# A fixed TensorE order in the recurrence groups of a bidirectional RWKV-7 layer: value products ahead of the lora-ups, bonus sums one key product later

## The chip, the cores and the metric

One core of a Trainium2 chip runs the whole kernel. The metric is the device time of one execution in microseconds. Five engines matter here: TensorE (PE, with its weight loads shown as PEld), VectorE (DVE), ScalarE (ACT), GpSimd (POOL), and SyncE (SP), whose queue issues most DMA transfers. Each engine works through its own list of instructions in order; semaphores tie the lists together.

## The reference

One layer over 2176 tokens (128 context tokens, 2048 latent ones) of 1024 channels. All tokens go through one input projection to eight groups of 512 channels. Four of them (r, k, v and a gate) feed an RWKV-7 recurrence, the other four a short convolution. For the recurrence the reference computes, cut to what matters here:

```python
proj = h @ lp['w_in']
r, k, v, g_a, b_gate, c_gate, u_conv, g_b = jnp.split(proj, IN_SPLITS, axis=-1)
rkv = _token_shift(jnp.concatenate([r, k, v], axis=-1), mu, is_latent)   # mixes each token with its two neighbours
lw = jnp.tanh(h @ decay_down);  w = decay_w0 + lw @ decay_up             # per direction
decay = jnp.exp(-jnp.exp(-softplus(-w) - 0.5))
a = sigmoid(iclr_bias + (h @ iclr_down) @ iclr_up)                       # per direction
kk = heads(k * kk_scale);  kk = kk * rsqrt(max(sum(kk * kk, -1), 1e-24))
kd = k * (1 + (a - 1) * ka_scale)                                        # per direction
# ... the recurrence itself, over r, decay, kd, v, kk, a ...
bonus = sum(r * kd * bonus_rk, axis=(direction, head channel))
y = y + bonus * v
```

## The kernel before

The kernel has a first phase, which makes the recurrence's operands and the convolution half and spills them to DRAM, and later phases, which run the recurrence and the output projection. Only the first phase is touched.

**Blocks, thirds, groups.** The tokens are cut into six blocks j of 384 tokens (the last has 256), and the blocks into three thirds of two (`THIRD`). For each third the loop goes over four groups g of 128 channels, and inside over the third's two blocks: `groupA(g, j, ...)` makes the recurrence operands of one group and block. There are 24 such calls. After the four groups of a third come its four convolution groups (`groupB`).

**A product** (`dense`) is a 128-channel slice of the projection for one block: eight slices of the 1024 input channels, three matmuls each (high and low parts of an fp32 split), so 24 matmuls into one PSUM tile. The tiles are named mmk, mmr, mmv and mmg for key, receptance, value and gate. The PSUM pool `pmm` has five buffers in turn, shared by these four and by the four lora-ups of a group (`up`, two matmuls each), eight tiles a group.

**A token shift** (`shifted`) evacuates a product: ScalarE copies it into a padded tile (rawl; for the context, which is in block 0, rawc too) and scales it (q1k, q1r, q1v), GpSimd adds the two neighbours (shk, shr, shv), and VectorE joins both (ok, or, ov, the shifted key, receptance and value).

**A part sum** (`part_sum`) adds the channels of each head with a matrix of ones: ScalarE copies the input to a high part (hsh), GpSimd subtracts it from the input (hsl, the low part), and TensorE does two matmuls. A group has two: the *key sum* pss of the squared key (sq, parts hshs and hsls), whose maximum and reciprocal VectorE takes for the normalised key; and the *bonus sum* psb of bs, a product of both directions' kd and the shifted receptance (parts hshb and hslb). bs is written into the first kd tile, so it shows as `kd<-kd,dv,or`.

**The rest of a group.** Per direction: tanh of the two lora-ups, a scan over 64 tokens (t), two exponentials (pp and t), and four operand tiles al, rh, ka and be, all with the tag "sp" and four buffers in turn, each spilled by a DMA from SP's queue; a ninth "sp" tile q takes bonus times value. Three transposes (psv) turn the value, VectorE subtracts its mean (vmean, vt) and vt is spilled. The low part of a part sum and vt share one buffer (tag "vt").

**Order.** A scheduler with a cost model of its own puts each engine's instructions in order from the program's order and its estimates, so that an engine's list need not follow the text. In the first third the weights are split into their parts when first loaded (`load_w`: a cast on ScalarE, a subtraction on VectorE) and written back; the later thirds read the parts.

Of the kernel before, what the change touches and what calls it, by code (L numbers as in the profile page):

```python
# [49 lines left out]
def phase1(K):  # L50
# [50 lines left out]
    def dcol(i):  # L101
        return dv[:, i:i + 1]
# [84 lines left out]
            q = 32 * (k % 4)  # L187
            T.matmul(ps[q:q + 32, :], scp[:, k, :], wt[:, i, :], start=k < 4, stop=k >= 4)

    def parts_of(t_, n, nm, eng):  # L190

        hi = ta_.tile([128, 384], F32R, tag="hsh", name=f"hsh{nm}", bufs=1)
        lo = ta_.tile([128, 384], F32R, tag="vt", name=f"hsl{nm}", bufs=1)
        P.copy(hi[:, :n], t_[:, :n])
        eng.tensor_tensor(lo[:, :n], t_[:, :n], hi[:, :n].bitcast(F32), ALU.subtract)  # L195
        return hi, lo

    def part_sum(o, t_, n, nm, eng=G):

        hi, lo = parts_of(t_, n, nm, eng)  # L200
        ps = pax.tile([128, 384], F32, tag="ax", name=f"ps{nm}")
        T.matmul(ps[:, :n], o[:], hi[:, :n], start=True, stop=False)
        T.matmul(ps[:, :n], o[:], lo[:, :n], start=False, stop=True)
        return ps
# [123 lines left out]
    def groupA(g, j, ws, hh, lw, pre):  # L328
# [8 lines left out]
        P.activation(sq[:, :n], kS[:, :n], AF.Square, scale=vcol(V_KK + g))  # L337
        pss = part_sum(onr, sq, n, f"s{g}_{j}")
# [4 lines left out]
        P.activation(kk[:, :n], kS[:, :n], AF.Identity, scale=vcol(V_KK + g))  # L343
        kkn = n2
        V.tensor_tensor(kkn[:, :n], kk[:, :n], n2[:, :n], ALU.mult)
        rS = shifted(psr or dense(wr_, hh, n, "r"), j, 0, g, "r", 1)
        kds = []
        for d in range(2):
            cs = slice(g * 128, g * 128 + 128)
# [23 lines left out]
            ta = tl("ta", 2)  # L373
            P.activation(ta[:, :n], psa[:, :n], AF.Tanh, bias=dcol(D_IBH + d * 4 + g), scale=0.5)  # L374
            v3 = lambda x_: x_[:, :n].rearrange("p (a b) -> p a b", b=64)
            al = tl("sp", 4)
            V.tensor_tensor(v3(al), v3(kk), pt[:, :nch, d:64 + d], ALU.mult)
            spill(f"al{d}", g, j, al, "al")
            rh = tl("sp", 4)
# [4 lines left out]
            kd = tl("kd", 2)  # L384
            P.activation(kd[:, :n], ta[:, :n], AF.Identity, bias=dcol(D_KA2 + g), scale=vcol(V_KA + g))
            V.tensor_tensor(kd[:, :n], kd[:, :n], kS[:, :n], ALU.mult)
            kap = tl("sp", 4)
            V.tensor_tensor(kap[:, :n], kd[:, :n], c[:, :n], ALU.mult)
            spill(f"ka{d}", g, j, kap, "kap")
            be = tl("sp", 4)  # L390
            V.scalar_tensor_tensor(be[:, :n], ta[:, :n], 1.0, kkn[:, :n], ALU.add, ALU.mult)
            V.tensor_tensor(be[:, :n], be[:, :n], c[:, :n], ALU.mult)
            spill(f"be{d}", g, j, be, "be")
# [1 line left out]
        bs = kds[0]  # L395
        V.tensor_tensor(bs[:, :n], kds[0][:, :n], kds[1][:, :n], ALU.add)
        V.scalar_tensor_tensor(bs[:, :n], bs[:, :n], dcol(D_RKQ + g), rS[:, :n], ALU.mult, ALU.mult)
# [18 lines left out]
        psg = dense(wg, hh, n, "g")  # L416
        tg = tl("sg", 2)
        P.activation(tg[:, :n], psg[:, :n], AF.Tanh, scale=0.5)
        sg = tg
        V.scalar_tensor_tensor(sg[:, :n], tg[:, :n], 1.0, psg[:, :n], ALU.add, ALU.mult)  # L420
        spill("sg", g, j, sg, "sg")
        q = tl("sp", 4)
        V.tensor_tensor(q[:, :n], psb[:, :n], vS[:, :n], ALU.mult)
        V.scalar_tensor_tensor(q[:, :n], q[:, :n], dcol(D_GBH + g), sg[:, :n], ALU.add, ALU.mult)
        spill("q", g, j, q, "q")

    def groupB(g, j, ws, hh):
        t0, n = BLK[j]
# [102 lines left out]
            yield  # L531

    up = {}

    def run(gen):
        for _ in gen:
# [990 lines left out]
```

## Time and profile before

| | |
|---|---|
| three timed runs | 1683.29 us median (1681.29 to 1694.95) |
| the profiled execution | 1692.05 us, span 1690.3 us |
| recurrence groups of the first, second, last third | 69 to 237, 405 to 590, 744 to 886 us |
| share of the span: PE, DVE, ACT, POOL | 91%, 68%, 47%, 31% |
| granted TensorE clock, mean | 0.964 |
| HBM traffic | 184 GB/s over the span |

The profile is of one execution. In its rows a group of instructions is named by line, engine, operation and tiles (out<-in); a wait is put down to what ended it. Matmuls overlap, so a matmul's duration is longer than the step from one to the next. A tile's name without numbers stands for all its buffers.

### The profile page before, as it was taken

To read this page: it belongs to the slowest core of one execution; us is meant where nothing else is said; L and a number is where in the kernel's file an instruction comes from. 1 tells how busy PE (TensorE), PEld (TensorE's weight loads), DVE (VectorE), ACT (ScalarE), POOL (GpSimd) and SP (SyncE) were. 2 spreads that over 40 slices of the span, in tenths; PEclk is the share of its full clock that TensorE was granted. 3 is DMA by queue.
4 is the path that set the end of the run, shared out by engine and by line. 5 is a ranking of instruction groups with operands and counts; after the bars stand their busy time and mean duration, and the time that the engine had idled before them with its cause. 6 is when DMAs were issued, how large, how long until landed. Compare 5 with 4: busy or idle time off the path is not lost.

```text
span 1690.3 us, 42026 instructions
## 1 busy us (share of the span) xinstructions
PE 1538.1 (91%) x17364; PEld 1416.5 (84%) x17364; DVE 1147.6 (68%) x2112; ACT 792.4 (47%) x1590; POOL 531.6 (31%) x952
## 2 busy tenths in 40 slices
PE   5898899999999899999999998998989897699998
PEld 2898899898888899999998997888888786577786
DVE  5988897644678744547876426798898887446433
ACT  4565554322355512225552106877867767422222
POOL 0032220000122200002321714788777775212221
PEclk9999999999999999999999998999999999899999
DMA  9688886664878763448877636566565754455442
GB/s 373 225 241 241 236 253 229 225 213 161 176 172 193 198 177 114 141 153 200 214 233 265 208 113 154 153 179 166 177 175 163 184 142 144 113 156 180 145 149 93
DMA packets 204591, 313.95 MB, mean 186 GB/s; under 512 B 58088, under 2 KB 147560, under 8 KB 190320
## 3 DMA queue, kind: packets, MB, share of 16 engines
q1 hardware_dynamic: 168816, 311.13, 61.1%
q10 hardware_dynamic: 35584, 0.14, 1.5%
q8 instruction: 136, 2.23, 0.6%
q14 instruction: 55, 0.45, 0.1%
HBM read 208.05 MB, written 103.17 MB: 184 GB/s over the span
## 4 chain that ended last, share of the span: by engine, by line
PE 46%; DVE 8%; DMA 7%; issue 3%; ACT 2%; POOL 0%; SPq 0%; DVEq 0%; ACTq 0%; POOLq 0%
PE psE L1066 6%; PE psS L1097 4%; PE psu L1381 3%; DMA scr_ops<-sp 3%; PE psu L1382 3%; PE psu L1383 3%; PE psFm L899 2%; PE psX L1048 2%; PE psGm L899 2%; PE mmb L160 1%; PE mmb L158 1%; PE mmb L159 1%; PE mmgb L159 1%; PE mmgb L160 1%; PE mmgb L158 1%
## 5 line engine op out<-in xcount | busy, mean ns | idle before, releaser
L971 POOL TENSOR_TENSOR zt<-zt,ztmp 128x30 f32<-128x30 f32 (+7 forms) x510 | 206.2, 404 | 39.7
L968 POOL TENSOR_TENSOR ztmp<-ab,zt 128x60 f32<-128x60 f32 (+7 forms) x255 | 137.2, 538 | 105.2 <-DVE ab L959 86.3
L1097 PE MATMUL psS<-sv,E 128*64 128x64 f32 x2176 | 103.1, 231 | 26.5 <-DVE so L1123 12.4
L1097 PEld LDWEIGHTS psS<-sv,E 128*64 128x64 f32 x2176 | 85.3, 141 | 46.1 <-issue 18.3
L314 POOL TENSOR_TENSOR shk<-rawl 128x384 f32<-128x384 f32 (+1 forms) x24 | 20.3, 845 | 274.8 <-ACT rawl L310 176.6
L1071 DVE TENSOR_TENSOR E<-psE,msk 128x512 f32<-128x512 f32 x136 | 91.0, 684 | 19.1 <-PE psE L1066 18.2
L1123 DVE TENSOR_TENSOR sv<-psS,pc 64x128 f32<-64x128 f32 x254 | 64.1, 275 | 42.4 <-PE psS L1097 40.8
L1446 POOL TENSOR_TENSOR z<-z,x 128x512 f32<-128x512 f32 x32 | 42.8, 1338 | 150.8 <-DVE z L1440 86.5
L158 PE MATMUL mmv<-h,w 128*128 128x384 f32 (+1 forms) x192 | 70.5, 367 | 19.6 <-ACT q1r L312 10.1
L1052 ACT ACTIVATE stf<-psX 64x512 f32<-64x512 f32 x136 | 80.5, 592 | 13.3 <-PE psX L1048 10.9
L159 PE MATMUL mmv<-h,w 128*128 128x384 f32 (+1 forms) x192 | 68.7, 358 | 0.0
L160 PE MATMUL mmv<-h,w 128*128 128x384 f32 (+1 forms) x192 | 68.5, 357 | 0.1
L195 POOL TENSOR_TENSOR hsls<-sq,hshs 128x384 fp32r<-128x384 f32 (+1 forms) x24 | 33.0, 1373 | 112.1 <-DMA scr_vt<-vt 39.5
L158 PE MATMUL mmg<-h,w 128*128 128x384 f32 (+1 forms) x192 | 63.2, 329 | 4.6 <-ACT ta L374 2.6
L158 PE MATMUL mmc<-h,w 128*128 128x384 f32 (+1 forms) x192 | 64.1, 334 | 0.5 <-DMA w<-scr_wsp 0.5
L159 PE MATMUL mmgb<-h,w 128*128 128x384 f32 (+1 forms) x192 | 63.5, 331 | 0.0
L158 PE MATMUL mmgb<-h,w 128*128 128x384 f32 (+1 forms) x192 | 63.5, 331 | 0.0
L160 PE MATMUL mmgb<-h,w 128*128 128x384 f32 (+1 forms) x192 | 63.2, 329 | 0.0
L159 PE MATMUL mmc<-h,w 128*128 128x384 f32 (+1 forms) x192 | 63.0, 328 | 0.0
L160 PE MATMUL mmb<-h,w 128*128 128x384 f32 (+1 forms) x192 | 62.8, 327 | 0.0
L160 PE MATMUL mmc<-h,w 128*128 128x384 f32 (+1 forms) x192 | 62.8, 327 | 0.0
L158 PE MATMUL mmu<-h,w 128*128 128x384 f32 (+1 forms) x192 | 62.7, 327 | 0.0
(311 smaller groups left out, 5114.4 us busy)
## 6 DMA issues: line engine op xcount, KB each, us to landing
w<-scr_wsp SPq DMA_DIRECT2D x68, 1024.0 KB, 6.8
scr_wsp<-w SPq DMA_DIRECT2D x34, 1024.0 KB, 6.1
rr<-scr_ops SPq DMA_DIRECT2D x32, 1024.0 KB, 5.6
scr_ops<-sp SPq DMA_DIRECT2D x160, 192.0 KB, 5.3
wr<-in_win SPq DMA_DIRECT2D x34, 512.0 KB, 7.0
x<-in_x SPq DMA_DIRECT2D x17, 512.0 KB, 3.6
wadas<-in_wada SPq DMA_DIRECT2D x8, 1024.0 KB, 14.8
sv<-scr_vt SPq DMA_DIRECT2D x32, 256.0 KB, 4.3
```

What stands on the lines that cost most here:

```text
L158: T.matmul(ps[:, :n], w[:, 0, k], hh[:, 0, k, :n], start=k == 0, stop=False)
L159: T.matmul(ps[:, :n], w[:, 0, k], hh[:, 1, k, :n], start=False, stop=False)
L160: T.matmul(ps[:, :n], w[:, 1, k], hh[:, 0, k, :n], start=False, stop=k == 7)
L899: T.matmul(dst(h, a, er), w[hr_, u, :], x(hr_, u), start=True, stop=True)
L968: G.tensor_tensor(tv, ab[:, j:j + 2, j + 2:32].unsqueeze(1).broadcast_to((128, kn, 2, n)), zt[:, :kn, j:j + 2].unsqueeze(3).broadcast_to(( ...
L971: G.tensor_tensor(zt[:, :kn, j + 2:32], zt[:, :kn, j + 2:32], tv[:, :, r], ALU.subtract)
L1052: P.activation(g.fs[64:128, :, hd, e::2], g.ps["X"][e][hr_].rearrange("p a (b t) -> p b a t", b=2), AF.Copy, scale=-1.0)
L1066: T.matmul(pe[r, i, hd, :].rearrange("p (b t) -> p b t", b=2), lt[:, b, hd, us.start + k + i], rt[:, :, hd, us.start + k + i], start=True, ...
L1071: V.tensor_tensor(g.E[n][:, k:k + 2].rearrange("p a b c -> p (a b) c"), pe[:].rearrange("p a b c -> p (a b) c"), B.msk[:, ME[g.d]].unsquee ...
L1097: T.matmul(g.sp[i // 4][r, q, hd, :], g.E[n][:, k, hd, r], g.sv[:, u, hd, :], start=True, stop=True)
L1123: V.tensor_tensor(dst, g.sp[i // 4][0:64, q], B.pc[0:64, d, 2 * p:2 * p + 2, c:c + 1].broadcast_to((64, 2, 64)), ALU.mult)
L1381: T.matmul(ps[:], mh[:, n], hi[:, cs], start=start and n == 0, stop=False)
```

## The change

Five edits, all in the first phase's recurrence groups:

1. Around each group's two blocks the scheduler is switched off for TensorE (`manual_schedule`), which then takes its instructions in program order.
2. In the program, receptance and value (product and shift) move up to right behind the key, ahead of the key sum and the lora-ups; the gate product moves up ahead of the value's transposes.
3. The bonus sum's two copies stay with the group, but its matmuls and q are put into `later` and come after the next group's key product (after the last group of a third, at its end).
4. The parts get homes of their own: the key sum's low part the tag "hsl", the bonus sum's two parts the tags "ob" and "bsv" of another pool, vt the tag "pv".
5. The "sp" tiles have five buffers instead of four.

```diff
-    def parts_of(t_, n, nm, eng):
-        hi = ta_.tile([128, 384], F32R, tag="hsh", name=f"hsh{nm}", bufs=1)
-        lo = ta_.tile([128, 384], F32R, tag="vt", name=f"hsl{nm}", bufs=1)
+    def parts_of(t_, n, nm, eng, home=None):
+        pool, th_, tl_ = home or (ta_, "hsh", "hsl")
+        hi = pool.tile([128, 384], F32R, tag=th_, name=f"hsh{nm}", bufs=1)
+        lo = pool.tile([128, 384], F32R, tag=tl_, name=f"hsl{nm}", bufs=1)
...
-        kS = shifted(psk or dense(wk, hh, n, "k"), j, 1, g, "k", 1)
+        psk = psk or dense(wk, hh, n, "k")
+        for f in later:
+            f()
+        later.clear()
+        kS = shifted(psk, j, 1, g, "k", 1)
+        psr = psr or dense(wr_, hh, n, "r")
+        rS = shifted(psr, j, 0, g, "r", 1)
+        psv_ = dense(wv, hh, n, "v")
+        vS = shifted(psv_, j, 2, g, "v", 1)
...
-        rS = shifted(psr or dense(wr_, hh, n, "r"), j, 0, g, "r", 1)
...
-            al = tl("sp", 4)
+            al = tl("sp", 5)
...
-        psb = part_sum(onr, bs, n, f"b{g}_{j}")
-        vS = shifted(dense(wv, hh, n, "v"), j, 2, g, "v", 1)
+        bp = parts_of(bs, n, f"b{g}_{j}", G, (tp, "ob", "bsv"))
+        psg = dense(wg, hh, n, "g")
...
-        vt = ta_.tile([128, 3, 128], F32, tag="vt", name=f"vt{g}_{j}", bufs=1)
+        vt = tp.tile([128, 3, 128], F32, tag="pv", name=f"vt{g}_{j}", bufs=1)
...
+        def bonus():
+            psb = sum_of(onr, bp, n, f"b{g}_{j}")
+            q = tl("sp", 5)
...
+        later.append(bonus)
...
+            order = tc.manual_schedule(engines={mybir.EngineType.PE})
+            order.__enter__()
             for j in js:
                 groupA(g, j, ws, hs[j], lws[j], pre.pop(j, None))
+            if g == 3:
+                for f in later:
+                    f()
+                later.clear()
+            order.__exit__(None, None, None)
```

`sum_of` is the second half of `part_sum`: the PSUM tile and the two matmuls.

How the lists of three engines change is shown at one place, the pass from block 2 to block 3 in the second group of the second third (`_2_` and `_3_` are the blocks). TensorE before, from the bonus sum of block 2 (psb) inside the key product of block 3:

```order
L202 MATMUL psb_2_4415<-hshb_2_4411,onr 128x384
L158 MATMUL mmk_4492<-h_3716,w_497_4261 128x384
L159 MATMUL mmk_4492<-h_3716,w_497_4261 128x384
L160 MATMUL mmk_4492<-h_3716,w_497_4261 128x384
L403 MATMUL psv_2_4450<-idt,ov_4448 128x128 x3
L203 MATMUL psb_2_4415<-hslb_2_4412,onr 128x384
```

The key product's other matmuls and the receptance product follow there; the key sum of block 3 stands behind receptance and lora-ups, and the value product behind its first matmul. TensorE now, at the end of the same key product:

```order
L159 MATMUL mmk_4502<-h_3728,w_496_4269 128x384
L160 MATMUL mmk_4502<-h_3728,w_496_4269 128x384
L206 MATMUL psb_2_4527<-hshb_2_4460,onr 128x384
L207 MATMUL psb_2_4527<-hslb_2_4461,onr 128x384
L158 MATMUL mmr_4541<-h_3728,w_497_4271 128x384
L159 MATMUL mmr_4541<-h_3728,w_497_4271 128x384
```

Both matmuls of the bonus sum now stand between key and receptance, and behind the receptance come the value product, the key sum, eight lora-up matmuls and the gate product, in this order in every group.

ScalarE now, at the same pass (sg is block 2's gate, t an exponential of block 2, hshb the bonus sum's copy, rawl and q1k the evacuation of block 3's key):

```order
L413 ACTIVATE sg_2_534_4489<-mmg_4464 128x384
L382 ACTIVATE t_2_525_4430<-t_2_525_4430,nln_111 128x384
L393 DMA scr_pc_60<-pp_0_475 128x6x1
L314 COPY rawl_466<-mmk_4502 128x6x64
L316 ACTIVATE q1k_4535<-mmk_4502,dv 128x384
L195 CAST hshb_2_4460<-kd_2_521_4417 128x384
L349 ACTIVATE sq_3_548_4605<-ok_4539,vec 128x384
L355 ACTIVATE kk_3_549_4616<-ok_4539,vec 128x384
L195 CAST hshs_3_4607<-sq_3_548_4605 128x384
```

The copy of bs stands behind both evacuations of the next key; before, it stood ahead of block 2's gate here, and behind the next key's evacuations in every second group.

VectorE before, from the scans of block 2 to its key sum's reciprocal (L396 and L397 make bs):

```order
L365 SCALAR_TENSOR_TENSOR t_2_512_4350<-smask,t_2_512_4350 128x384
L386 TENSOR_TENSOR kd_2_517_4368<-kd_2_517_4368,ok_4299 128x384
L367 SCALAR_TENSOR_TENSOR t_2_521_4381<-smask,t_2_521_4381 128x384
L386 TENSOR_TENSOR kd_2_526_4399<-kd_2_526_4399,ok_4299 128x384
L377 TENSOR_TENSOR sp_2_515_4361<-kk_2_506_4312,pp_0_474 128x384
L380 TENSOR_TENSOR sp_2_516_4364<-or_4345,pp_0_474 128x384
L388 TENSOR_TENSOR sp_2_518_4371<-kd_2_517_4368,t_2_512_4350 128x384
L396 TENSOR_TENSOR kd_2_517_4368<-kd_2_517_4368,kd_2_526_4399 128x384
L397 SCALAR_TENSOR_TENSOR kd_2_517_4368<-kd_2_517_4368,dv,or_4345 128x384
L340 TENSOR_SCALAR sq_2_505_4301<-pss_2_4307 128x384
L320 SCALAR_TENSOR_TENSOR ov_4448<-shv_4446,dv,q1v_4444 128x384
L341 RECIPROCAL sq_2_505_4301<-sq_2_505_4301 128x384
```

VectorE now, from bs of block 2 to the scans of block 3, and then from block 3's first operand to its bs:

```order
L408 SCALAR_TENSOR_TENSOR kd_2_521_4417<-kd_2_521_4417,dv,or_4348 128x384
L324 SCALAR_TENSOR_TENSOR ok_4539<-shk_4537,dv,q1k_4535 128x384
L403 TENSOR_TENSOR sp_2_532_4454<-sp_2_532_4454,t_2_525_4430 128x384
L435 TENSOR_TENSOR sp_2_536_4530<-psb_2_4527,ov_4380 128x384
L436 SCALAR_TENSOR_TENSOR sp_2_536_4530<-sp_2_536_4530,dv,sg_2_534_4489 128x384
L324 SCALAR_TENSOR_TENSOR or_4571<-shr_4569,dv,q1r_4567 128x384
L352 TENSOR_SCALAR sq_3_548_4605<-pss_3_4611 128x384
L353 RECIPROCAL sq_3_548_4605<-sq_3_548_4605 128x384
L324 SCALAR_TENSOR_TENSOR ov_4603<-shv_4601,dv,q1v_4599 128x384
L376 SCALAR_TENSOR_TENSOR t_3_551_4622<-smask,t_3_551_4622 128x384
L357 TENSOR_TENSOR sq_3_548_4605<-kk_3_549_4616,sq_3_548_4605 128x384
L397 TENSOR_TENSOR kd_3_556_4640<-kd_3_556_4640,ok_4539 128x384
```

```order
L388 TENSOR_TENSOR sp_3_554_4633<-kk_3_549_4616,pp_0_474 128x384
L391 TENSOR_TENSOR sp_3_555_4636<-or_4571,pp_0_474 128x384
L399 TENSOR_TENSOR sp_3_557_4643<-kd_3_556_4640,t_3_551_4622 128x384
L402 SCALAR_TENSOR_TENSOR sp_3_558_4646<-ta_3_553_4631,sq_3_548_4605 128x384
L388 TENSOR_TENSOR sp_3_563_4664<-kk_3_549_4616,pp_0_475 128x384
L415 SCALAR_TENSOR_TENSOR sg_3_569_4712<-sg_3_569_4712,mmg_4687 128x384
L428 TENSOR_REDUCE vmean_3_4721<-psv_3_4716 128x6
L407 TENSOR_TENSOR kd_3_556_4640<-kd_3_556_4640,kd_3_565_4671 128x384
L403 TENSOR_TENSOR sp_3_558_4646<-sp_3_558_4646,t_3_551_4622 128x384
L429 SCALAR_TENSOR_TENSOR vt_3_4720<-vmean_3_4721,psv_3_4716 128x384
L391 TENSOR_TENSOR sp_3_564_4667<-or_4571,pp_0_475 128x384
L408 SCALAR_TENSOR_TENSOR kd_3_556_4640<-kd_3_556_4640,dv,or_4571 128x384
```

The maximum and reciprocal of the key sum moved from behind bs to ahead of the scans, and bs from ahead of them to the end of its group's operands. In the second third's first block (2) the last operands, ka and be of the second direction, stand ahead of bs too.

More of the change, by code (lines that the diff above doesn't have):

```diff
@@ L198, in part_sum, with sum_of @@
     def part_sum(o, t_, n, nm, eng=G):
-        hi, lo = parts_of(t_, n, nm, eng)
+        return sum_of(o, parts_of(t_, n, nm, eng), n, nm)
+    def sum_of(o, parts, n, nm):
+        hi, lo = parts
         ps = pax.tile([128, 384], F32, tag="ax", name=f"ps{nm}")
@@ L375, in groupA @@
             v3 = lambda x_: x_[:, :n].rearrange("p (a b) -> p a b", b=64)
-            al = tl("sp", 4)
+            al = tl("sp", 5)
             V.tensor_tensor(v3(al), v3(kk), pt[:, :nch, d:64 + d], ALU.mult)
             spill(f"al{d}", g, j, al, "al")
-            rh = tl("sp", 4)
+            rh = tl("sp", 5)
             V.tensor_tensor(v3(rh), v3(rS), pt[:, :nch, 1 - d:65 - d], ALU.mult)
@@ L386, in groupA @@
             V.tensor_tensor(kd[:, :n], kd[:, :n], kS[:, :n], ALU.mult)
-            kap = tl("sp", 4)
+            kap = tl("sp", 5)
             V.tensor_tensor(kap[:, :n], kd[:, :n], c[:, :n], ALU.mult)
             spill(f"ka{d}", g, j, kap, "kap")
-            be = tl("sp", 4)
+            be = tl("sp", 5)
             V.scalar_tensor_tensor(be[:, :n], ta[:, :n], 1.0, kkn[:, :n], ALU.add, ALU.mult)
@@ L397, in groupA @@
         V.scalar_tensor_tensor(bs[:, :n], bs[:, :n], dcol(D_RKQ + g), rS[:, :n], ALU.mult, ALU.mult)
-        psb = part_sum(onr, bs, n, f"b{g}_{j}")
-        vS = shifted(dense(wv, hh, n, "v"), j, 2, g, "v", 1)
+        bp = parts_of(bs, n, f"b{g}_{j}", G, (tp, "ob", "bsv"))
+        psg = dense(wg, hh, n, "g")
+        tg = tl("sg", 2)
+        P.activation(tg[:, :n], psg[:, :n], AF.Tanh, scale=0.5)
+        sg = tg
+        V.scalar_tensor_tensor(sg[:, :n], tg[:, :n], 1.0, psg[:, :n], ALU.add, ALU.mult)
+        spill("sg", g, j, sg, "sg")
         psv = pax.tile([128, 3, 128], F32, tag="ax", name=f"psv{g}_{j}")
@@ L414, in groupA @@
         nc.sync.dma_start(S["vt"][t0:t0 + n, g * 128:(g + 1) * 128].rearrange("(a p) c -> p a c", p=128), vt[:, :n // 128])
[L416 to L425, printed above, removed]
+        def bonus():
+            psb = sum_of(onr, bp, n, f"b{g}_{j}")
+            q = tl("sp", 5)
+            V.tensor_tensor(q[:, :n], psb[:, :n], vS[:, :n], ALU.mult)
+            V.scalar_tensor_tensor(q[:, :n], q[:, :n], dcol(D_GBH + g), sg[:, :n], ALU.add, ALU.mult)
+            spill("q", g, j, q, "q")
+        later.append(bonus)
     def groupB(g, j, ws, hh):
@@ L533, in phase1 @@
     up = {}
+    later = []
     def run(gen):
```

## The prediction

> **What bounds the kernel now.** I read the page first, then the busy time by stretches, then TensorE's waits, then VectorE's timeline. The three stretches are the recurrence groups of the three thirds, from the first product or lora-up to the last gate product. Columns: span, then busy us of PE, PEld, DVE, ACT, POOL, granted clock, DMA share, GB/s.
>
> ```profile
> PE 1538.1 (91%) x17364; PEld 1416.5 (84%) x17364; DVE 1147.6 (68%) x2112; ACT 792.4 (47%) x1590; POOL 531.6 (31%) x952
> 69.05:236.60 167.55, 150.60 (x835) 146.64 (x835) 149.03 (x223) 101.70 (x199) 43.81 (x36) 0.97 0.85 245
> 405.33:590.47 185.14, 165.04 (x885) 159.90 (x885) 133.87 (x206) 89.61 (x183) 40.86 (x39) 0.94 0.75 178
> 743.64:886.01 142.37, 134.22 (x881) 131.59 (x880) 108.71 (x193) 79.12 (x175) 36.29 (x38) 0.98 0.74 200
> ```
>
> TensorE leads with 91%, and in these 495 us too it is the busiest engine; but VectorE is close behind (149 of 168 us in the first third). What TensorE waits for there:
>
> ```profile
> PE psb L202 <- ACT hshb L194: 15.1, 8, 2.8
> PE mmv L158 <- ACT q1r L312: 10.1, 6, 4.0
> PE mmv L158 <- ACT rawc L317: 9.5, 3, 4.2
> PE pss L202 <- ACT hshs L194: 5.0, 3, 2.1
> PE mmg L158 <- ACT ta L374: 2.6, 2, 1.7
> ```
>
> Columns: total, times, longest. The first four, 39.7 us, are the waits that the new order could remove. Over 24 groups that is under 2 us a group. A wait costs more than its length once it is long (columns: idle or product stretch, PE busy, clock, DMA):
>
> ```profile
> 186.61:191.06 4.45, 4.45 (x25) 1.00 1.00 389
> 201.13:203.63 2.50, 0.00 (x1) 1.00 0.89 193
> 203.63:209.64 6.01, 6.01 (x24) 0.72 0.82 276
> 468.84:475.40 6.56, 6.56 (x24) 0.62 0.25 83
> ```
>
> 24 matmuls take 4.45 us at full clock, after the 1.7 us wait for ta, and 6.01 us after TensorE had stood still for 2.50 us: 1.6 us lost. After 4 us of idling it was about 2 us.
>
> **The change: TensorE's part.** A key, receptance, value or gate product of 384 columns is 24 matmuls; from first to last of both widths:
>
> ```profile
> 503.50 0.33 PE L158 MATMUL mmr<-h,w 128*128 128x384 f32 x1
> 507.66 0.34 PE L355 MATMUL up<-lw,ups 128*128 128x384 f32 x1
> 764.93 0.28 PE L158 MATMUL mmr<-h,w 128*128 128x256 f32 x1
> 767.81 0.28 PE L355 MATMUL up<-lw,ups 128*128 128x256 f32 x1
> ```
>
> So 4.16 us at 384 columns and 2.88 at 256. The number of matmuls doesn't change: four products, eight lora-ups, four sums and three transposes, 19.0 us a group (13.1 at 256). What changes is what stands in front of what. TensorE now goes key, bonus sum of the group before, receptance, value, key sum, lora-ups, gate. Receptance and value cannot start until the bonus sum has both its copies, and the lora-ups and the key sum stand behind them.
>
> **What the bonus sum waits for.** ScalarE's order puts its copy (hshb) behind the two evacuations of the next key product, and GpSimd's difference (hslb) comes after it. In every group but each third's last, whose bonus sum stands among later products. Durations:
>
> ```profile
> L310 ACT COPY rawl<-mmk 128x384 f32<-128x384 f32 x8 | 3.8, 481 | 27.3 <-PE mmk L160 27.3
> L312 ACT ACTIVATE q1k<-mmk,dv 128x384 f32<-128x384 f32 x8 | 4.7, 588 | 0.0
> L194 ACT CAST hshb<-kd 128x384 fp32r<-128x384 f32 x7 | 3.6, 513 | 25.8 <-DVE kd L397 25.8
> L195 POOL TENSOR_TENSOR hslb<-kd,hshb 128x384 fp32r<-128x384 f32 x7 | 8.0, 1136 | 30.0 <-ACT hshb L194 28.8 <-PE pss L203 1.3
> ```
>
> Even with the input ready, TensorE stops 0.5+0.5+0.5+1.1+0.3 = 2.9 us after each key product. But the input, bs (kd, L397 before, L408 now), is not ready. VectorE's order now is: key sum's maximum, reciprocal, value shift, scans, kd, operands, and only near the end bs; before, bs stood ahead of the maximum. The rows:
>
> ```profile
> 493.08 0.96 DVE L365 TENSOR_TENSOR_SCAN t<-smask,t 128x384 f32<-128x384 f32 x1 [1.34 <-ACT t L362]
> 493.95 0.53 DVE L386 TENSOR_TENSOR kd<-kd,ok 128x384 f32<-128x384 f32 x1
> 496.11 0.53 DVE L386 TENSOR_TENSOR kd<-kd,ok 128x384 f32<-128x384 f32 x1
> 496.56 0.55 DVE L377 TENSOR_TENSOR sp<-kk,pp 128x384 f32<-128x384 f32 x1
> 497.49 0.55 DVE L340 TENSOR_SCALAR sq<-pss 128x384 f32<-128x384 f32 x1
> 498.08 2.55 DVE L341 RECIPROCAL sq<-sq 128x384 f32<-128x384 f32 x1
> 500.55 0.50 DVE L388 TENSOR_TENSOR sp<-kd,t 128x384 f32<-128x384 f32 x1
> 500.96 0.61 DVE L320 SCALAR_TENSOR_TENSOR ov<-shv,dv,q1v 128x384 f32<-128x384 f32 x1
> 501.48 0.55 DVE L345 TENSOR_TENSOR sq<-kk,sq 128x384 f32<-128x384 f32 x1
> 878.01 0.54 DVE L412 TENSOR_REDUCE vmean<-psv 128x6 f32<-128x384 f32 x1
> 880.81 0.55 DVE L392 TENSOR_TENSOR sp<-sp,t 128x384 f32<-128x384 f32 x1
> L367 DVE TENSOR_TENSOR_SCAN t<-smask,t x24: 673/948/1781, 77.3 to 891.0; 128x384 f32<-128x384 f32 x20, 128x256 f32<-128x256 f32 x4
> L397 DVE SCALAR_TENSOR_TENSOR kd<-kd,dv,or x24: 380/611/1357, 83.8 to 897.9; 128x384 f32<-128x384 f32 x20, 128x256 f32<-128x256 f32 x4
> ```
>
> From start to start: maximum 0.59, reciprocal 2.47, value shift 0.52, scan 0.87 (twice; the second at its median, 0.95 long), kd 0.45 (twice), kk 0.47: 6.7 us. Short ones follow each other every 0.47 us (six steps from 878.01 to 880.81). In the second third, 13 of them stand ahead of bs when the block is the first of its pair, 11 when it is the second; bs itself is 0.6. From the key sum's end to bs: 13.4 and 12.5 us. TensorE meanwhile does lora-ups, gate, transposes and next key, 10.1 us, and then stands.
>
> **The loop.** bs, copy and difference and first sum (0.5+1.1+0.4 = 2.0), receptance and value and key sum (2x4.16+0.5 = 8.8), then VectorE again: 24.2 us (second block 23.3). No engine can run ahead around it. To it come the clock's loss, since TensorE stands 5 to 6 us each time, and the landing of operand writes: the sixth sp of a burst takes the first one's buffer (there are five), ten short starts less its own 0.55 us, so 4.1 us, after that was written.
>
> ```profile
> DMA to landing us min/median/max: 1.7/5.0/12.3
> ```
>
> At the median, with 0.2 to issue, that is a wait of 1.1 us; its ends as a mean are 0 (landing in 1.7) and some 2 (a landing of 6). The clock costs 1.6, between 0 (the 186.61 row, after 1.72 us of idling) and 2.0 (the 468.84 row); I take 1.6, since every wait here exceeds 2.50 us.
>
> **The sum by thirds.** Second third: start to key sum 13.0, four loops of 26.9 and three of 26.0, then 5.8 for lora-ups, gate, transposes: 204.4 against 185.1. Minus 4 for the last group's stop in the products behind (the 2.8 us of the psb row and its lost clock), which the later place avoids: **+15**.
>
> First third: VectorE also splits weights and adds the context's edge; the second block's chain has two weight splits of 1.2, an edge add of 0.3 and the next key's shift of 0.5 ahead of bs, but ten short ones, and its sixth sp comes behind bs.
>
> ```profile
> L128 DVE TENSOR_TENSOR w<-wr,w x34: 1156/1221/2054, 21.9 to 358.4; 128x1024 fp32r<-128x1024 f32 x34
> 76.80 0.49 ACT L546 ACTIVATE lf<-mml 128x384 f32<-128x384 f32 x1 [0.62 <-DVE lw L551]
> 82.80 0.62 ACT L337 ACTIVATE sq<-ok,vec 128x384 f32<-128x384 f32 x1 [2.60 <-DVE lw L551]
> ```
>
> Chains of 13.2 and 15.2, loops of 26.7 and 27.6: 189.6. The first key sum is late as well: its square (82.80 before) shares a buffer with lf and waits for its four parts, behind lf at about 76; square, copy, difference and sum then end near 81, and TensorE stands some 7 us with the lora-ups behind it. 81+189.6+5.8 = 276.4 against 236.6: **+40**.
>
> Last third: blocks of 384 and 256 columns. The 384 chain is 13.7, followed by receptance and value at 256 (6.2): 13.7+2.0+6.2+1.6+1.1 = 24.6. The 256 chain has nine short ones ahead of bs; at the products' ratio of 0.69 it is 8.0, then 1.4+8.8+1.6: 19.8. 13.0+157.8+4.1 = 174.9 against 142.4: **+32**.
>
> Together +87. The profiled execution was 1692 us (span 1690.3), 9 above the median of 1683.3; I add 87 to the median: **1770 us**.
>
> **Edits that cost nothing here.** The fifth sp buffer and the copies' own homes only take waits away; I price their gain in the landing term, not again. The next weight load stands on SP's queue ahead of four operand writes and waits for the second block's key product, but that ends 10.1 us into the chain, and the first of those operands is ready after 11; uncovered, each us late would be a us of the sp wait. The gate product needs the value's evacuation, 0.5+0.6 us, covered by 1.4 us of lora-ups.
>
> **Rivals.** (A) The forecast. (B) *Only the copy's place costs*: bs is ready before the key product ends. TensorE then stops 2.9 us a boundary and loses 1.6 two times in three, as I count it (2.50 us lost it, 1.72 did not, and these 2.9 come in two pieces): 23.0 a loop. Second third 13+161+5.8 against 185.1, minus 4: -9; first 81+161+5.8: +11; last (3.5 pairs of 39.3, and 17): +12. Sum +14: 1697. For it: the waits for hshb are already the longest kind. Against it: 13.4 against 10.1 us. (C) The same without the clock's loss: 21 losses of 1.1 fewer, -22 on B, 1675. The row at 203.63 speaks against it: 2.50 us of idling was enough.
>
> By the Trainium skill, "TensorE: Matmul & The Clock Gate", section "HAM oscillation — how this bites in real kernels", the rule is "no PE-idle gaps >~3.4µs". By it B's stops would cost no clock, and B would become C, 1675 instead of 1697; this case's trace disagrees at 2.50 us. A's stops exceed both bounds, so its sum is the same.
>
> (D) *Faster*: the stop at the bonus sum is short or none, because the copies come in time. Loops of 19.0: -37, -17 and -13 in the thirds, 1616. It decides at the key product's end: bs must come under 8 us after the key sum instead of 13, and its copy ahead of the evacuations. Both orders speak against it; only durations that shrink by nearly half could do it. (E) That the change doesn't do what it says: one block's transposes stand inside the next key product instead of before it, which moves 0.5 us and no wait.
>
> **How the numbers follow.** A 0.82, B 0.08, C 0.04, D 0.06. A's own range: without clock loss (21 loops) and landing waits (15) it is +37, with 2.0 and 2 each +109, and a VectorE slowed beside GpSimd (scans of up to 1.78 instead of 0.95 in the row above) can add some: 1720 to 1810. The range is carried to B, 1696 to 1810, and leaves out C, D and what exceeds A. Faster by over 1% is D, 0.06; within 1% (17 us; the three runs spread over 14) B and C, 0.12; slower 0.82.
>
> **What would show it.** Right: receptance matmuls waiting for GpSimd's hslb (their bonus sum with them) 20-odd times, 5 to 7 us in all each; VectorE idle until pss, then a burst of 12 to 15 us that ends in bs; a granted clock near 0.9 or less in the three stretches, which grow to about 207, 204 and 175 us; the waits of mmv for q1r and rawc gone. Wrong: hshb on ScalarE without a wait for bs, which is B, or stretches of 150 us, which is D; a burst much longer than 15 us with waits for scr_ops would put the time above the range.

## The result and the profile after

The changed kernel takes **1850.1 us** (median of 4 runs, 1847.3 to 1853.6) against 1688.7 for the kernel before in the same comparison: ratio **1.096, interval 1.093 to 1.099**. The direction was forecast, the size was not: 1770 with a range to 1810. The page's first line:

```profile
PE 1567.5 (85%) x17364; PEld 1441.1 (78%) x17364; DVE 1118.3 (60%) x2112; ACT 789.9 (43%) x1590; POOL 521.8 (28%) x952
```

TensorE, busy for 91% of the span before, is so for 85% of a longer one. The same three stretches as before, from the first product or lora-up to the last gate product, with the columns of the first table (span, busy us of PE, PEld, DVE, ACT, POOL, clock, DMA share, GB/s):

```profile
69.05:295.83 226.78, 167.81 (x839) 159.99 (x838) 144.81 (x233) 103.64 (x205) 43.88 (x37) 0.86 0.70 186
468.05:709.20 241.15, 172.08 (x885) 166.80 (x885) 124.25 (x202) 89.93 (x181) 38.76 (x39) 0.84 0.55 134
862.56:1048.30 185.74, 140.58 (x884) 136.36 (x883) 105.78 (x202) 79.24 (x180) 30.41 (x39) 0.88 0.63 164
```

The stretches grew by 59.2, 56.0 and 43.4 us: 158.6 of the span's 159.9. Everything happened where the order changed. TensorE's waits (total, times, longest):

```profile
PE psb L206 <- ACT hshb L195: 150.0, 22, 11.3
PE psb L207 <- POOL hslb L196: 17.1, 21, 2.2
```

The waits of mmv for q1r and rawc are gone. In their place TensorE stands at the bonus sum in nearly every group, 6.8 us for the copy and 0.8 for the difference. VectorE's waits:

```profile
DVE sp L391 <- DMA scr_ops<-sp: 118.8, 24, 9.1
DVE or L324 <- POOL shr L318: 102.0, 23, 7.0
DVE sq L352 <- PE pss L207: 34.9, 21, 2.5
```

The first row is the surprise: in every one of the 24 groups it stops at an operand tile, 5.0 us each time, until an earlier tile has been written out. One pass of the second third in VectorE's timeline, from the key sum's maximum to bs (start, duration, idle before it in brackets):

```profile
511.89 0.56 DVE L352 TENSOR_SCALAR sq<-pss 128x384 f32<-128x384 f32 x1 [2.42 <-PE pss L207]
...
518.49 0.55 DVE L388 TENSOR_TENSOR sp<-kk,pp 128x384 f32<-128x384 f32 x1
...
522.70 0.55 DVE L429 SCALAR_TENSOR_TENSOR vt<-vmean,psv 128x384 f32<-128x384 f32 x1
531.51 0.56 DVE L391 TENSOR_TENSOR sp<-or,pp 128x384 f32<-128x384 f32 x1 [8.26 <-DMA scr_ops<-sp]
531.99 0.61 DVE L408 SCALAR_TENSOR_TENSOR kd<-kd,dv,or 128x384 f32<-128x384 f32 x1
```

and the copy and the bonus sum behind it, in ScalarE's and TensorE's:

```profile
532.63 0.51 ACT L195 CAST hshb<-kd 128x384 fp32r<-128x384 f32 x1 [9.65 <-DVE kd L408]
533.20 0.69 PE L206 MATMUL psb<-hshb,onr 128*128 128x384 f32 x1 [11.27 <-ACT hshb L195]
```

The burst runs without a pause for 11 us, stands for 8.3, and bs comes 20.7 us after the maximum began. The tile made first (518.49) must land before the sixth can be made. Just ahead of its write, issued at 519.07, ScalarE issues two writes of the chunk factors pc:

```profile
517.10 0.37 ACTq L393 DMA_DIRECT2D scr_pc<-pp  x1
518.73 0.37 ACTq L393 DMA_DIRECT2D scr_pc<-pp  x1
```

Time to landing of that one operand write:

```profile
DMA to landing us min/median/max: 12.4/12.4/12.4
```

And the engines, clock, DMA share and GB/s of the four us behind its issue:

```profile
519.00:523.00 4.00, 2.93 (x18) 2.58 (x17) 4.00 (x10) 1.53 (x4) 0.42 (x1) 1.00 0.73 49
```

The DMA engines were 73% busy, and moved 49 GB/s.

### The profile page after: what moved, and what is told of

The parts are those of the page before. It is cut to its first block, busy times and chain, and to the rows that moved or that the text cites. A ratio compares the mean times of both kernels' runs of the same rounds, so it can differ in the third digit from the quotient of the medians.

```text
span 1850.2 us, 42083 instructions
## 1 busy us (share of the span) xinstructions
PE 1567.5 (85%) x17364; PEld 1441.1 (78%) x17364; DVE 1118.3 (60%) x2112; ACT 789.9 (43%) x1590; POOL 521.8 (28%) x952
## 4 chain that ended last, share of the span: by engine, by line
PE 57%; issue 15%; DMA 11%; DVE 10%; ACT 3%; POOL 3%; SPq 1%; DVEq 0%; POOLq 0%; ACTq 0%
DMA scr_ops<-sp 7%; PE psE L1088 5%; PE psS L1119 3%; PE psu L1403 3%; PE psu L1404 3%; PE psu L1405 3%; PE psFm L921 2%; PE psGm L921 2%; PE psX L1070 2%; PE mmgb L160 2%; PE mmb L158 2%; PE mmb L159 2%; PE mmgb L158 2%; PE mmgb L159 1%; PE mmb L160 1%
## 5 line engine op out<-in xcount | busy, mean ns | idle before, releaser
L318 POOL TENSOR_TENSOR shk<-rawl 128x384 f32<-128x384 f32 (+1 forms) x24 | 26.3, 1095 | 415.5 <-ACT rawl L314 415.5
L206 PE MATMUL psb<-hshb,onr 128*128 128x384 f32 (+1 forms) x24 | 14.7, 611 | 150.0 <-ACT hshb L195 150.0
L206 PEld LDWEIGHTS psb<-hshb,onr 128*128 128x128 f32 x24 | 6.3, 262 | 156.6 <-ACT hshb L195 156.6
L391 DVE TENSOR_TENSOR sp<-or,pp 128x384 f32<-128x384 f32 (+1 forms) x48 | 25.6, 534 | 118.8 <-DMA scr_ops<-sp 118.8
L324 DVE SCALAR_TENSOR_TENSOR or<-shr,dv,q1r 128x384 f32<-128x384 f32 (+1 forms) x24 | 15.0, 624 | 102.0 <-POOL shr L318 102.0
L158 PE MATMUL mmr<-h,w 128*128 128x384 f32 (+1 forms) x184 | 75.2, 408 | 0.0
L196 POOL TENSOR_TENSOR hslb<-kd,hshb 128x384 fp32r<-128x384 f32 (+1 forms) x24 | 31.9, 1327 | 151.1 <-ACT hshb L195 151.1
L159 PE MATMUL mmr<-h,w 128*128 128x384 f32 (+1 forms) x184 | 74.0, 402 | 0.0
L160 PE MATMUL mmr<-h,w 128*128 128x384 f32 (+1 forms) x184 | 72.9, 396 | 0.0
L160 PE MATMUL mmv<-h,w 128*128 128x384 f32 (+1 forms) x192 | 62.8, 327 | 3.2 <-DVE w L128 3.2
L465 ACT ACTIVATE sg<-mmgb 128x384 f32<-128x384 f32 (+1 forms) x24 | 11.4, 474 | 125.8 <-PE mmgb L160 125.8
```

The lines of the kernel that those rows point to most:

```text
L158: T.matmul(ps[:, :n], w[:, 0, k], hh[:, 0, k, :n], start=k == 0, stop=False)
L159: T.matmul(ps[:, :n], w[:, 0, k], hh[:, 1, k, :n], start=False, stop=False)
L160: T.matmul(ps[:, :n], w[:, 1, k], hh[:, 0, k, :n], start=False, stop=k == 7)
```

## The experiments

Eleven kernels. Ratios are to the kernel before, run beside each on the same chip.

**What makes the operand writes land late.** `pt[:, :nch, 64 - 64 * d]` has a stride, so each of the 48 pc writes is 768 pieces of 4 bytes (512 at block 5).

```
-            nc.scalar.dma_start(S[f"pc{d}"][rows, chunks], pt[:, :nch, 64 - 64 * d])
+            P.copy(pcs[:, d, g, chunks of the third], pt[:, :nch, 64 - 64 * d])
...                                     # behind the third's four groups
+            nc.scalar.dma_start(S[f"pc{d}"], for all g, pcs[:, d])
```

> The changed kernel, but the chunk factors pc are copied by ScalarE into one tile and written once a third (pieces of 48 bytes, 6 writes in all) instead of 48 writes of 4-byte pieces. Theory L (the 4-byte writes, two of them just ahead of the burst's operand writes, make those land late, and the sixth operand tile waits for the first to land): the operand writes land in 2 to 4 us, VectorE's wait for scr_ops at the rh line falls from 118.8 us to under 25, the loops of the second third from 32.1 to 26-27 us, the total to 1755 (1735 to 1775). Rival W (the 1 MB weight loads ahead of the burst, or six 192 KB writes in a row, make them late): the wait stays over 80 us in sum and the total over 1815. Rival C (the chain or the clock is longer than assumed, the landing beside the point): the wait goes and the total stays over 1815.

1773.9 us, ratio 1.054 (1.051 to 1.057). The stretches:

```profile
69.05:277.28 208.23, 165.74 (x843) 159.73 (x842) 146.13 (x233) 105.17 (x219) 43.13 (x37) 0.88 0.58 202
446.23:651.60 205.37, 173.42 (x885) 168.64 (x885) 125.66 (x202) 91.94 (x195) 44.10 (x39) 0.89 0.47 157
800.14:974.75 174.61, 143.81 (x884) 139.60 (x883) 107.78 (x202) 81.22 (x194) 30.30 (x39) 0.89 0.52 175
```

VectorE's remaining wait for operand writes at the same line:

```profile
  DVE sp L391: 15.5, 9
```

Theory L: the wait fell from 118.8 to 15.5 us, and all nine waits that are left stand behind bs; the loops of the second third (key sum to key sum) fell to 25.1 to 27.6 us (26.7 in the mean), the time by 76, to the upper end of the forecast. The weight loads and the row of operand writes are all still there, so W alone is out. Beside the short pieces a weight load does count: in the changed kernel's second third, the waits of second blocks, whose operand write was issued 1.6 us behind a weight load, were 6.5 to 8.3 us, those of first blocks, without one, 3.0 to 4.0.

A pass in the middle of the second third, with pc written once a third, shows what the DMA engines do with the same burst. First the landing of its first operand write, issued at 599.39, then the stretch behind that, then VectorE's maximum, sixth tile and bs:

```profile
DMA to landing us min/median/max: 4.0/4.0/4.0
```

```profile
599.40:606.00 6.60, 3.32 (x19) 2.71 (x17) 6.60 (x14) 1.82 (x5) 1.50 (x2) 0.98 0.99 358
```

```profile
592.21 0.56 DVE L352 TENSOR_SCALAR sq<-pss 128x384 f32<-128x384 f32 x1 [2.45 <-PE pss L207]
...
603.49 0.71 DVE L391 TENSOR_TENSOR sp<-or,pp 128x384 f32<-128x384 f32 x1
604.12 0.61 DVE L408 SCALAR_TENSOR_TENSOR kd<-kd,dv,or 128x384 f32<-128x384 f32 x1
```

358 GB/s over these 6.6 us (341 in the first four) instead of 49, a landing of 4.0 us instead of 12.4, and no idle time ahead of the sixth tile. Is it the number of writes or that of their pieces?

```
-            nc.scalar.dma_start(S[f"pc{d}"][rows, chunks], pt[:, :nch, 64 - 64 * d])
+            P.copy(pcs[:, :nch], pt[:, :nch, 64 - 64 * d])
+            nc.scalar.dma_start(S[f"pc{d}"][rows, chunks], pcs[:, :nch])
```

> The changed kernel, its 48 pc writes kept at their places, but from a compact copy by ScalarE, so that each is 128 pieces of 24 bytes (at block 5, 16) instead of 768 of 4 bytes. Theory P (the number of short pieces is what holds up the operand writes behind them): a sixth of the pieces, landing waits at the rh line down from 118.8 us to 10-40, total 1775 to 1800. Rival S (every short write costs the same whatever the number of its pieces, or the write's place counts): waits near 119 us, 1835 to 1855.

1772.4 us, 1.053 (1.049 to 1.056): as good as leaving them to the end, and just below the range of theory P. The pc and operand writes of the changed kernel (KB each, median us to landing):

```profile
scr_ops<-sp SPq DMA_DIRECT2D x160, 192.0 KB, 5.5
scr_pc<-pp ACTq DMA_DIRECT2D x40, 3.0 KB, 6.6
```

and of this run:

```profile
scr_ops<-sp SPq DMA_DIRECT2D x160, 192.0 KB, 2.8
scr_pc<-pcs ACTq DMA_DIRECT2D x40, 3.0 KB, 2.4
```

The same 3 KB at the same place, in 128 pieces instead of 768, land in 2.4 us, and VectorE's wait at the sp row is as short as with six writes in all (15.8 us, 9 times, against 15.5). So it is the cutting into single elements. As the bytes stay the same, the number of pieces and their size change together, and no run here tells these two apart. A second way by which they could act is in the trace of the changed kernel too, SP's queue waiting for a pc write before it issues an operand write:

```profile
SPq L330 <- DMA scr_pc<-pp: 39.2, 19, 4.9
```

Both edits take that away as well, but the writes that VectorE waits for did not wait so: the one above was issued as soon as its tile was made, at 519.07, and of the 24, 23 were issued 0.03 us after their tile was made and one 0.35 us.

**What the clock costs.** Idle matmuls fill the stop:

```
+        if warm:
+            for i in range(48):
+                T.matmul(ps[:, :256], w[:, 0, i % 8], hh[:, 0, i % 8, :256], start=True, stop=True)
         T.matmul(ps[:, :n], o[:], hi[:, :n], start=True, stop=False)
```

> The changed kernel, and ahead of each deferred bonus sum 48 idle matmuls of 256 columns (some 5.8 us at full clock, into the sum's own PSUM tile, overwritten by it) that keep TensorE busy while the copies are awaited. If the clock's loss after each stop is a term of the loop (1.6 to 2.0 us in 20-odd loops), receptance's 24 matmuls go back from 6.3 to 4.3 us and the total falls by 30 to 45 us, to 1805-1820. If the loss is beside the critical path, or the stop outlasts the idle matmuls by over 2 us and the clock falls anyway: 1840 to 1860.

1831.3 us, 1.088 (1.085 to 1.092): 19 less, outside both forecasts. The stretches say why:

```profile
69.05:282.10 213.05, 192.71 (x1173) 186.55 (x1172) 143.58 (x232) 103.60 (x205) 39.49 (x37) 0.98 0.74 198
457.24:686.18 228.94, 205.05 (x1221) 201.40 (x1221) 123.51 (x202) 89.92 (x181) 38.79 (x39) 0.95 0.57 141
839.43:1031.83 192.40, 179.19 (x1219) 176.87 (x1218) 105.49 (x202) 79.56 (x180) 30.55 (x39) 0.95 0.60 159
```

13.7 and 12.2 us gained in the first two thirds, 6.7 lost in the last, where every second loop (19.4 us) has no stop to fill and 48 matmuls made it 22.8. I had counted the gain there too. Again, without the landings, with 32 of them and only between blocks of 384:

> The run with pc written once a third (1773.9 us), and 32 idle matmuls of 256 columns (some 3.9 us) ahead of each deferred bonus sum between two blocks of 384 columns. There receptance took 6.3 us from first to last matmul behind the stops of 4 to 5 us against 4.16 at full clock. If that is the clock after the stop: 4.2 to 4.9 us, and 15 loops each 1.4 to 2.1 us shorter: 1742 to 1755. If receptance is slow for another reason (the transfers, the operands): no change, 1768 to 1780.

1754.4 us, 1.045 (1.040 to 1.050), 19 below the run without them. One kernel shows both cases, since the stop that was left differs from block to block. TensorE's timeline at two passes of the first third:

```profile
147.39 0.44 PE L209 MATMUL psb<-hshb,onr 128*128 128x384 f32 x1 [0.29 <-ACT hshb L195]
148.70 0.44 PE L210 MATMUL psb<-hslb,onr 128*128 128x384 f32 x1 [0.87 <-POOL hslb L196]
...
173.38 0.45 PE L209 MATMUL psb<-hshb,onr 128*128 128x384 f32 x1 [1.79 <-ACT hshb L195]
174.46 0.53 PE L210 MATMUL psb<-hslb,onr 128*128 128x384 f32 x1 [0.63 <-POOL hslb L196]
```

and the receptance product behind each (span, PE busy, and the clock third from the end):

```profile
148.98:153.20 4.22, 4.22 (x26) 4.22 (x26) 2.20 (x3) 0.73 (x2) 1.01 (x1) 1.00 0.74 248
174.80:180.55 5.75, 5.75 (x26) 5.75 (x25) 2.99 (x6) 1.13 (x2) 1.12 (x1) 0.72 0.68 240
```

After 0.29 and 0.87 us of idling receptance runs at clock 1.00 in 4.2 us; after 1.79 and 0.63, at 0.72 in 5.75. The loops with the short stop take 24.6 us, those with the long one 27.3, as without idle matmuls. The loss is the clock's, and it is on the path. The length of the stop does not settle it alone: in the second third of this run four stops were nearly alike, 0.65 to 0.72 us ahead of the copy's matmul and 0.86 to 0.87 us ahead of the difference's. Two lost the clock and two did not; one of each:

```profile
562.64:566.88 4.24, 4.24 (x25) 4.24 (x25) 1.18 (x2) 0.00 (x0) 0.99 (x1) 1.00 0.74 286
611.31:617.07 5.76, 5.76 (x26) 5.76 (x25) 1.18 (x2) 0.00 (x0) 0.97 (x1) 0.70 0.58 213
```

**Where the fixed order goes wrong.** First without it:

```
-            order = tc.manual_schedule(engines={mybir.EngineType.PE})
-            order.__enter__()
...
-            order.__exit__(None, None, None)
```

> The changed kernel without the fixed order on TensorE (edit 1 undone; the code order, the deferred bonus sum, the copies' homes and the fifth operand buffer stay). The planner then puts both halves of the bonus sum mostly among later products. If the fixed order is the cause (nothing can run past a waiting sum): 1685 (1660 to 1705). Rival (the bonus sum deferred past the key product, with VectorE's bs behind the next key sum, is the cause in any order): 1740 or above.

1681.8 us, 0.9995 (0.9977 to 1.0014): without the fixed order the whole loss is gone; in the planner's order the products' new places, the later bonus sum, the homes and the fifth buffer together cost nothing. Then with it, but the deferred sum two products further down:

```
-        for f in later: ...             # behind the key product
         psv_ = dense(wv, hh, n, "v")
+        for f in later: ...             # behind the value product
```

> The changed kernel, but the deferred bonus sum stands behind the next group's value product instead of behind its key product, so receptance and value no longer wait for its copies. Forecast's loop: key sum, burst of 13.4 plus the landing wait of 4 to 5, copies 2.0, bonus sum and key sum 0.9: 21 us against TensorE's own 19.0, so 21 to 22 in place of 32.1 in the second third, and some 190 us less in all: 1660 (1630 to 1700). Rival (ScalarE's copy stays behind all six evacuations of key, receptance and value, or the gate product's place matters more): loops of 25 and more, 1730 or above.

1724.1 us, 1.024 (1.021 to 1.028): between the two forecasts, with loops of 21.4 to 25.7 us in the second third. The landing wait is still there, and it now stands ahead of the next key's shift on VectorE, which the key sum needs. VectorE's and TensorE's waits:

```profile
DVE sp L391 <- DMA scr_ops<-sp: 80.4, 23, 6.4
```

```profile
PE pss L206 <- ACT hshs L195: 25.7, 14, 5.4
```

I had added it to the burst only, not to what stands behind the burst. With both edits, the sum behind the value product and pc written once a third:

> Fixed order on TensorE, deferred bonus sum behind the value product, and pc written once a third. With the 4-byte writes the same order had loops of 23.6 us in the second third, and VectorE's 5 us wait for the landing stood in front of the shift that the key sum needs. Theory (a fixed order costs only what stands late at its waiting row; copy leg and landing were all of it): loops of 19 to 20.5, TensorE's own 19.0 with little idle, total 1640 (1625 to 1660). Rival (any fixed order pays, one late input stops all): 1680 or above.

1647.1 us, **0.981 (0.977 to 0.985)**; loops of 19.1 to 19.6 us in the second third, in which TensorE is idle for 0.7 us in all:

```profile
399.54:553.86 154.32, 153.66 (x885) 152.45 (x885) 128.17 (x201) 92.36 (x195) 40.93 (x39) 1.00 0.59 208
```

In that third a fixed order as such costs nothing. What cost in the changed kernel was one row that waits in it, with 24 matmuls of each of two products behind it that could have run.

**The rest of the change, and the 4-byte writes in the kernel before.** Edits 4 and 5 alone on the kernel before:

```
-        lo = ta_.tile([128, 384], F32R, tag="vt", name=f"hsl{nm}", bufs=1)
+        lo = ta_.tile([128, 384], F32R, tag="hsl", name=f"hsl{nm}", bufs=1)
...      # vt = tp.tile(..., tag="pv"); tl("sp", 4) -> tl("sp", 5)
```

> The kernel before with edits 4 and 5 alone: the differences and vt in places of their own, a fifth operand buffer; order of code, of TensorE and bonus sum as before. Priced in the prediction as nothing but waits taken away: 1676 (1666 to 1684). Rival (a planner that sees other release times moves TensorE's rows and the gain or loss is its): outside these bounds.

1692.5 us, 1.006 (1.004 to 1.009): a small loss where I had a small gain, so the rival. TensorE's rows are in another order, and the stretches are 163.1, 179.0 and 157.3 us instead of 167.6, 185.1 and 142.4: gained in two thirds, lost in the last. pc written once a third, on the kernel before:

> The kernel before with pc kept in one tile and written once a third. There VectorE waited some 60 us for operand buffers, but TensorE, the bound, only 40 us for anything in the three stretches. Theory (landing waits are mostly hidden behind TensorE in the order of before): 1676 (1668 to 1683). Rival (they set the times of the bonus and key sums' inputs there too): 1665 or less.

1639.3 us, **0.973 (0.970 to 0.976)**: theory wrong by 37 us. I had read TensorE's named waits only. Its second third before was 185.14 us with 165.04 busy at clock 0.94; now:

```profile
395.93:556.80 160.87, 155.59 (x884) 153.31 (x884) 137.16 (x207) 90.86 (x199) 39.49 (x39) 0.99 0.60 203
```

14.8 us less idle, and at clock 0.99 9.5 less busy. Both on top of each other:

> The kernel before with pc written once a third (1639.3 us) and edits 4 and 5 on top. Alone on the kernel before these two edits made 1692.5 of 1684.7. If they only take waits away, and what they cost there came from the landings that their other planned order met: 1639 (1632 to 1645). If the planner's other order costs in itself: 1646 or more.

1632.5 us, 0.971 (0.967 to 0.974), not to be told from 0.973 by these intervals: the homes' loss is gone with the landings. And the changed kernel without the fixed order, with pc written once a third:

> The changed kernel without TensorE's fixed order (1681.8 us) and with pc written once a third. There VectorE waits 52.8 us for the landing of operand writes, 16 times. Theory (that wait feeds the sums that TensorE waits for, 28 us in all): 1660 (1648 to 1672), the first version below both kernels. Rival (TensorE is busy beside it): 1675 to 1685.

1626.3 us, **0.967 (0.964 to 0.970)**, the fastest of all, and far below what I expected, by the same error as in the kernel before.

```profile
69.20:219.37 150.17, 145.37 (x833) 143.18 (x833) 144.79 (x224) 101.38 (x212) 39.65 (x36) 1.00 0.74 268
390.99:548.27 157.28, 154.95 (x885) 153.72 (x885) 122.51 (x199) 91.85 (x193) 44.47 (x39) 0.99 0.59 204
696.80:830.18 133.38, 131.46 (x879) 129.72 (x878) 108.83 (x194) 80.01 (x190) 37.29 (x38) 0.99 0.60 215
```

TensorE is busy for all but 9 of these 441 us, at clock 0.99 to 1.00.

With pc written once a third, then, no fixed order here is a gain: the best one takes 1647.1 us, the kernel before 1639.3, the planner's order of the changed kernel 1626.3. In the second third the best fixed order is ahead of the planner's (154.3 against 157.3 us), but in the first and the last it is behind (161.5 against 150.2, and 145.9 against 133.4). The two also differ in the place of the bonus sum, and why the first and the last third lose was not tried. The 0.981 is the pc writes' gain, not the order's.

## Why the prediction was right in kind and wrong in size

**The loop: right.** TensorE's fixed order, VectorE's burst with bs at its end, and copies that come after it form a ring that no engine can run ahead of. With no landing wait left ahead of bs, the run with pc written once a third is that ring by itself: stretches of 208.2, 205.4 and 174.6 us, where the sum's were 207.4 (276.4 less 69), 204.4 and 174.9. That they meet so closely is in part luck: the sum's 586.7 hold 16.5 of landing waits ahead of bs, which this run has not, so the rest of the sum was some 18 us short. The nine waits behind bs, 15.5 us, come near to that, but how much of them the loops feel was not taken apart. The chain from the maximum to the end of bs took 12.5 us in the pass shown (592.21 to 604.73), as in the sum. The first key sum, forecast for 81, ran at 79.7 and 80.8.

**The landing wait: the term that failed.** The sum had 1.1 us in 15 loops, 16.5 in all, with 2 as the upper end; the trace has 118.8, 5.0 us in all 24 groups. The step that failed is "At the median": it took the median of all writes to these tensors, 5.0 us, for the one write that the sixth tile waits for. That write is no typical one. ScalarE issues the group's two pc writes just ahead of it, and the trace of before already held the case: operand writes issued at 475.39 and 497.13 us, one after the other:

```profile
DMA to landing us min/median/max: 8.0/8.0/8.0
DMA to landing us min/median/max: 11.1/11.1/11.1
```

Of the operand writes of before whose landing the trace has, the 18 issued less than 2 us behind a pc write had a median of 7.8 us, the 58 with none in the 6 us before them 2.7. Weight loads do not make this difference: of the writes with no load issued in the 6 us before them either, 10 behind a pc write had a median of 7.3 us, 35 without one 1.9. At 7.8 the same sum (0.2 to issue, less 4.1) gives a wait of 3.9, not 1.1; in 15 loops that is 42 us more, and a forecast of 1812. In the event the 15 waits ahead of bs took 59.9 us (8.7, 36.2 and 15.0 in the thirds), 4.0 each. Of the nine others eight stand behind bs and one in a last group; I had counted them at nothing.

In the last third that held: its 256-column loops took 19.4 us, forecast 19.8. But that they came so close was luck. The sum had 1.6 us of clock loss in each, since "every wait here exceeds 2.50 us", and there was none: in all three TensorE stood for 1.40 and 0.42 us, and receptance took 4.18 us at clock 1.00. In the first of them bs was ready at 910.65, and its copy began at 911.69, when ScalarE had evacuated the next key. That is rival C's case: the copy's place alone costs, and no clock is lost.

In the first third the count of nothing did not hold: waits of 7.8 to 9.1 us behind the second block's bs push the operands that follow into the next block's chain, and the first block's loops took 30.8 to 32.6 us, forecast 26.7, and 27.1 to 28.1 with pc written once a third. The stretches missed the sum's by 67 us: 43 are the waits ahead of bs, some 15 those behind it (four loops that are 19.6 us longer, less the 4.3 of their own waits that are in the 43), the rest, some 9 us, was not taken apart.

**The clock's loss: right in kind, somewhat small.** Receptance behind the 14 stops at 384 columns takes 5.3 to 6.8 us from first to last matmul, 6.0 in the mean against 4.16: 1.9 each, where I took 1.6 with 2.0 as the end. (The row of 4.45 us that I read as 24 matmuls holds 25, the next key's first among them. The row of 6.01 runs to the last one's end. From first start to last, the 24 take 4.1 and 5.7 us, so the loss of 1.6 stands.) Over 14 stops that is 4 us more. The two runs with idle matmuls show that it is on the path. By the Trainium skill, "TensorE: Matmul & The Clock Gate", section "HAM oscillation — how this bites in real kernels", gaps up to some 3.4 us would be free; this case disagrees, since 1.79 and 0.63 us in two pieces cost 1.5, and 0.65 and 0.87 us did so in one pass.

**The rivals.** B and C would have had bs ready when the evacuations end, and so it was in the 256-column loops alone; in the pass shown ScalarE had done both by 523.0 and waited 9.65 us for bs. D needed bs 8 us after the key sum; it came after 12.5 and 20.7 in the two passes shown. "A burst much longer than 15 us with waits for scr_ops would put the time above the range" is what happened; I named the case and gave it too little room, since the ends of the term, 0 and 2, were those of a mean and not of that write.

**Edits that cost nothing.** The homes and the fifth buffer are neutral once landings are short (0.971 against 0.973), though alone on the kernel before they cost 0.6%: an edit that only frees buffers still has a price where the planner moves rows upon it. The 4 us expected behind the last group did not show: outside the three stretches the span grew by 1.3 us.

## What to carry to other kernels

Before an order is fixed by hand, ask of each waiting row what stands behind it that could run, and follow the ring back to the same row: here one sum moved behind two more products made the difference between 1.054 and 0.981. Where a term of a sum is a transfer, look up the very transfer that the chain waits for, with what was issued ahead of it, not the median of its kind. And a strided write of single elements is a suspect wherever a write behind it is waited for: gathering it first, into one write a third, was worth 3 to 4% in the kernel before and in the changed one, with the fixed order and without; in the changed kernel a contiguous copy at each write's own place did as much.

## What the runs showed of the hardware

Short pieces hold up other transfers far beyond their own time. The DMA view of 517 to 523 us in the changed kernel, from 2.1 us ahead of the burst's first operand write (packets; then each queue's packets, MB and share of 16 engines):

```profile
DMA packets 818, 0.28 MB, mean 47 GB/s; under 512 B 784, under 2 KB 784, under 8 KB 784
q1 hardware_dynamic: 34, 0.28, 63.6%
q10 hardware_dynamic: 784, 0.00, 6.0%
```

and of the same place, 597.3 to 603.3 us, with pc written once a third:

```profile
DMA packets 455, 1.49 MB, mean 248 GB/s; under 512 B 41, under 2 KB 327, under 8 KB 327
q1 hardware_dynamic: 455, 1.49, 73.6%
```

The 784 short pieces themselves took 6.0% of the engines' time, but the 34 pieces of 8 KB beside them 63.6% of 16 engines in 6 us, 1.8 us each. These 34 belong to the weight load, of 128 such pieces, that SP's queue issues 1.6 us ahead of the operand write; no piece of the operand writes, which are of 1.5 KB, starts before 525 us. In the other stretch all 128 pieces of the load started, and the operand writes' behind them; from 599.5 to 601.5 us, where the load's pieces run alone, 93 of them took 0.36 us each.

The operand writes' own pieces are slowed as well: in the changed kernel, from 555 to 557 us, behind two pc writes and with no load's pieces between, 52 pieces, 50 of them of 1.5 KB, took 0.55 us each; with pc written once a third, from 603 to 604.5 us, 435 pieces, 385 of them of 1.5 KB, took 0.06 us each.

The Trainium skill, "DMA: Bandwidth & Descriptors", section "Specifications", states that below 512 B a transfer falls from line rate because it reads before it writes. That would explain slow pc writes; that the load and the large writes issued around them stall is what the runs add, and 128 pieces of 24 bytes, also below 512 B, did it so little that it cost no time. What inside the memory or the engines stalls, no run here shows.
